# Splitting the first load of a row-mean kernel into eight DMAs of every eighth partition

## Chip, cores, metric

One core of one Trainium2 chip. The metric is device time of one execution in microseconds (us). "Span" is the time from the first to the last instruction in the profiled execution; it is some 2 us shorter than the device time. Every run in this document ran in the fast state at full clock. The kernel before repeats within some 0.3 us (one of its 46 runs beside the other kernels was 0.6 us above its median), so that differences of tenths of a us can be read when they recur. Profile views are cut to the lines that matter; code is cut where a comment says so.

## The reference

```python
def setup_inputs():
    batch, dim = 1024, 4096
    return {"x": np.random.randn(batch, dim).astype(np.float32), "axis": -1}

def reference(x, axis):
    mean = np.mean(x, axis=axis, keepdims=True)
    return ((x - mean) ** 2).astype(np.float32)
```

16.78 MB come in and 16.78 MB go out, with two cheap passes over the data between: it is a job for the DMA engines.

## The kernel before

Four rows of the input lie side by side in one partition, so that one half of the input is a tile of 128 partitions with 64 KiB in each. There are two such tiles; both are loaded at once, and each is stored in two halves as soon as its rows are done.

```python
    P, Q, H = 128, 4, 2
    ntiles = B // (P * Q)                       # 2
    x_t = x.rearrange("(n p q) d -> n p (q d)", p=P, q=Q)
    # ... out_t likewise, pools cut ...
    for i in range(ntiles):
        x_tile = io.tile([P, Q * D], F32)       # 128 x 16384: 64 KiB in each partition
        nc.sync.dma_start(out=x_tile, in_=x_t[i])
        tiles.append(x_tile)

    for i in range(ntiles):
        for q in range(Q):
            row = tiles[i][:, q * D:(q + 1) * D]
            # neg_sum = -sum(row) on VectorE; neg_mean = neg_sum / D; row = Square(row + neg_mean) on ScalarE (cut)
            if q % H == H - 1:
                part = slice((q + 1 - H) * D, (q + 1) * D)
                nc.sync.dma_start(out=out_t[i][:, part], in_=tiles[i][:, part])
```

Of the kernel before, what the change touches and what calls it, by code (L numbers as in the profile page):

```python
# [2 lines left out]

os.environ.setdefault("NEURON_RT_ULTRASERVER_MODE", "4")

# [4 lines left out]

F32 = mybir.dt.float32


@with_exitstack
def kernel(
    ctx: ExitStack,
    tc: tile.TileContext,
    x: bass.AP,
    axis: bass.AP,
    out: bass.AP,  # L20
):


    nc = tc.nc

    B, D = x.shape
    P = nc.NUM_PARTITIONS
    Q = 4
    H = 2
    assert B % (P * Q) == 0  # L30
    ntiles = B // (P * Q)
    inv_d = 1.0 / float(D)

    x_t = x.rearrange("(n p q) d -> n p (q d)", p=P, q=Q)
    out_t = out.rearrange("(n p q) d -> n p (q d)", p=P, q=Q)

    io = ctx.enter_context(tc.tile_pool(name="io", bufs=ntiles))
    stats = ctx.enter_context(tc.tile_pool(name="stats", bufs=2 * ntiles * Q))

    tiles = []  # L40
    for i in range(ntiles):
        x_tile = io.tile([P, Q * D], F32)
        nc.sync.dma_start(out=x_tile, in_=x_t[i])  # L43
        tiles.append(x_tile)

    for i in range(ntiles):
        for q in range(Q):
            row = tiles[i][:, q * D:(q + 1) * D]
            neg_sum = stats.tile([P, 1], F32)
            neg_mean = stats.tile([P, 1], F32)  # L50
            nc.vector.reduce_sum(  # L51
                out=neg_sum, in_=row, axis=mybir.AxisListType.X, negate=True
            )
            nc.vector.tensor_scalar_mul(out=neg_mean, in0=neg_sum, scalar1=inv_d)  # L54
            nc.scalar.activation(  # L55
                out=row,
                in_=row,
                func=mybir.ActivationFunctionType.Square,
                bias=neg_mean,
                scale=1.0,  # L60
# [6 lines that stand above are left out]
# [1 line left out]
_INS = ['x', 'axis']  # L68
_OUTS = [((1024, 4096), 'float32')]

_NUMBERS = {'axis': -1}


# [26 lines left out]
```

## Time and profile before

| | before |
|---|---|
| device time, median of 3 runs | 83.3 us (83.25 to 83.38) |
| span | 81.3 us |
| busy: VectorE, ScalarE | 35.4 us, 30.7 us |
| share of the DMA engines' time filled by packets | 96.2% |
| first load landed, second load landed (start of the reduction that waits for it) | 22.50 us, 41.83 us |
| one load packet (one partition's 64 KiB, on one of 16 DMA engines) | 2.418 us, 27.1 GB/s |

Read it from the last row upwards. Sixteen engines at 27.1 GB/s make 434 GB/s, and 33.55 MB at that rate take 77.3 us of the 81.3. The packet times come from the trace's records of single transfers; sixteen packets run side by side, and I call sixteen of them a *round*. A load is eight rounds. Nothing but the stream of rounds sets the time.

### The profile page before, as it was taken

The numbers are of one execution on the slowest core, as the hardware profiler recorded it, in microseconds if no ns is written. First come the engines' busy times: TensorE is split into PE (matmuls) and PEld (weight loads), VectorE is DVE, ScalarE is ACT, GpSimd is POOL, SyncE is SP. The second block draws the span as 40 slices with busy tenths as digits, with TensorE's granted clock in tenths as the row PEclk, the third lists the DMA queues.
The fourth block names the chain that finished last, engine by engine and source line by source line (L and its number), as shares of the span: only waits on it lengthen the run. The fifth ranks groups of instructions, "written<-read, shape, count | busy, mean of one in ns | idle before, by whom it ended". The sixth has DMA issues, their size and how long they took to land.

```text
span 81.3 us, 79 instructions
## 1 busy us (share of the span) xinstructions
DVE 35.4 (44%) x16; ACT 30.7 (38%) x9; POOL 0.2 (0%) x4
## 2 busy tenths in 40 slices
DVE  0000000000099999999749999999920000000000
ACT  0000000000060005969699930979879980000000
POOL 0000000000000000000000000000000000000000
DMA  9399947999965999992997997997998998898990
GB/s 387 129 516 516 516 193 322 516 516 516 516 290 226 516 516 516 516 483 129 419 516 306 467 516 322 451 516 338 435 516 354 419 516 387 387 516 387 403 500 0
DMA packets 864, 33.55 MB, mean 413 GB/s; under 512 B 96, under 2 KB 96, under 8 KB 96
## 3 DMA queue, kind: packets, MB, share of 16 engines
q1 hardware_dynamic: 864, 33.55, 96.2%
HBM read 16.78 MB, written 16.78 MB: 412 GB/s over the span
## 4 chain that ended last, share of the span: by engine, by line
DMA 50%; DVE 22%; ACT 5%; ACTq 4%; SPq 0%; issue 0%
DMA x_tile<-in_x_dram 50%; DVE neg_sum L51 21%; ACT x_tile L55 5%; ACTq L95 4%; SPq L43 0%; DVE neg_mean L54 0%
## 5 line engine op out<-in xcount | busy, mean ns | idle before, releaser
L51 DVE TENSOR_REDUCE neg_sum<-x_tile 128x1 f32<-128x4096 f32 x8 | 35.0, 4413 | 24.1 <-DMA x_tile<-in_x_dram 24.1
L55 ACT ACTIVATE x_tile<-x_tile,neg_mean 128x4096 f32<-128x4096 f32 x8 | 29.4, 3704 | 13.5 <-DVE neg_mean L54 13.5
L55 ACT ACT_TABLE_LOAD x1 | 1.3, 1283 | 22.5 <-DMA x_tile<-in_x_dram 22.5
L54 DVE TENSOR_SCALAR neg_mean<-neg_sum 128x1 f32<-128x1 f32 x8 | 1.1, 148 | 0.0
L81 POOL MEMSET const-bfloat16-1.0<- 128x1 bf16 x1 | 0.1, 101 | 0.0
L81 POOL MEMSET const-uint8-127<- 128x1 uint8 x1 | 0.1, 101 | 0.0
L81 POOL MEMSET const-float32-0.0<- 128x1 f32 x1 | 0.1, 98 | 0.2 <-issue 0.2
L81 POOL MEMSET const-float32-1.0<- 128x1 f32 x1 | 0.1, 98 | 0.0
## 6 DMA issues: line engine op xcount, KB each, us to landing
out_dram<-x_tile SPq DMA_DIRECT2D x4, 4096.0 KB, 12.9
x_tile<-in_x_dram SPq DMA_DIRECT2D x2, 31.2
```

What stands on the lines that cost most here:

```text
L51: nc.vector.reduce_sum(out=neg_sum, in_=row, axis=mybir.AxisListType.X, negate=True)
L54: nc.vector.tensor_scalar_mul(out=neg_mean, in0=neg_sum, scalar1=inv_d)
L55: nc.scalar.activation(out=row, in_=row, func=mybir.ActivationFunctionType.Square, bias=neg_mean, scale=1.0,)
L81: nc = _bacc.Bacc("TRN2", target_bir_lowering=False, num_devices=1)
L95: with _tile.TileContext(nc) as tc:
```

## The change

The first of the two loads becomes eight DMAs. DMA number g takes partitions g, g+8, ..., g+120: sixteen rows of 64 KiB, one for each DMA engine. The bytes, the row length and the number of rows per engine stay as they were; a plausible intent is to have many transfers in flight while each keeps all sixteen engines at work and spans the whole tile.

```diff
     H = 2
+    G = 8
@@
         x_tile = io.tile([P, Q * D], F32)
-        nc.sync.dma_start(out=x_tile, in_=x_t[i])
+        if i == 0:
+            for g in range(G):
+                nc.sync.dma_start(out=x_tile[g::G, :], in_=x_t[i][g::G, :])
+        else:
+            nc.sync.dma_start(out=x_tile, in_=x_t[i])
         tiles.append(x_tile)
```

## The prediction

It was written before the changed kernel had run. Its main account, to which it gives some 0.85, assumes that the sixteen rows of a small DMA share by twos the rate of one row (27.1 GB/s). That was the author's estimate: no trace of the kernel before shows it, where every row from the second round on takes 2.42 us.

> **What bounds the kernel now.** I read the page first, from the top down to the chain that ended last.
>
> ```profile
> span 81.3 us, 79 instructions
> DVE 35.4 (44%) x16; ACT 30.7 (38%) x9; POOL 0.2 (0%) x4
> ...
> DMA  9399947999965999992997997997998998898990
> GB/s 387 129 516 516 516 193 322 516 516 516 516 290 226 516 516 516 516 483 129 419 516 306 467 516 322 451 516 338 435 516 354 419 516 387 387 516 387 403 500 0
> ...
> q1 hardware_dynamic: 864, 33.55, 96.2%
> HBM read 16.78 MB, written 16.78 MB: 412 GB/s over the span
> ```
>
> No compute engine is busy half of the span, while the packets of the one DMA queue fill 96.2% of the sixteen transfer engines' time. The low digits in the two DMA rows are no gaps: a whole round of packets is booked at its end. In the trace's own packet records, the 256 load packets (65,536 B each) follow one another without a hole on every engine, 2.418 us each after a first round of 3.06 us, and the store packets (32,768 B, 1.213 us each) follow the last load at once, up to 80.2 us. So the kernel is one unbroken stream of 33.55 MB. Next I asked who waits for it, then the timeline.
>
> ```profile
> DVE neg_sum L51 <- DMA x_tile<-in_x_dram: 24.1, 2, 22.5
> ...
> SPq L64 <- ACT x_tile L55: 43.1, 4, 16.9
> SPq L64 <- DMA x_tile<-in_x_dram: 20.9, 1, 20.9
> ```
>
> ```profile
> 0.73 0.86 SPq L43 DMA_DIRECT2D x_tile<-in_x_dram  x2
> 22.50 8.75 DVE L51 TENSOR_REDUCE neg_sum<-x_tile 128x1 f32<-128x4096 f32 x2 [22.50 <-DMA x_tile<-in_x_dram]
> ...
> 39.46 27.65 SPq L64 DMA_DIRECT2D out_dram<-x_tile  x4
> ...
> 41.83 8.75 DVE L51 TENSOR_REDUCE neg_sum<-x_tile 128x1 f32<-128x4096 f32 x2 [1.62 <-DMA x_tile<-in_x_dram]
> ```
>
> Both loads are issued by 1.6 us. The first lets VectorE start at 22.50 us, the second at 41.83 us. The difference, 19.33 us for 8.39 MB, is 434 GB/s: the full rate of the stream. The first store is issued at 39.46 us, 2.4 us before the second load has ended, so it queues behind it. Compute sits between the loads and the stores but never starves the queue; the end is set by bytes over rate. A change matters only if it slows the stream or opens a hole in it.
>
> [...]
>
> **The change part by part.** *What stays.* The same 128 rows of 64 KiB, 8 per engine, the same bytes; every compute instruction; the stores. The instruction order of the two kernels differs on SyncE alone: eight 16-partition copies replace one of 128. In its waits, the first reduction, the table load and the first store now wait for eight semaphores, and the second load waits for the first small one, whose semaphore it reuses.
>
> *Issue.* The two issues on the timeline took 0.86 us, 0.43 each. Seven more are 7 x 0.43 = 3.0 us, all but the first beside transfers that are running: an engine's row takes at least 2.42 us, the next issue is there after 0.43. On the path: 0. The second load is issued after the first small one has landed[...], when each engine has about six rows still to do. On the path: 0.
>
> *Waits.* Seven more semaphore waits ahead of the first reduction[...] go into the 2.4 us by which the first store is early. On the path: 0.
>
> [...]Here is the cost. DMA number g writes partitions g, g+8, ..., g+120. [...] An engine works its rows in order, so the sixteen stay in step[...]. [...]two rows need 2 x 2.418 = 4.84 us. Eight rounds: 8 x 4.84 = 38.7 us against 8 x 2.418 = 19.3 us in the kernel before. Cost: +19.3 us, all of it on the path, since the stream has no hole. The first reduction moves from 22.5 to about 41.9 us, the second load's end from 41.8 to about 61, and stores follow it as now; the first store stays some 2 us ahead of it.
>
> *Sum.* 83.3 + 19.3 + 0 = 102.6 us. I take off 0.2: the engines start 0.5 us apart (packet starts 1.75 to 2.27 us in the trace)[...]. Predicted 102.4 us.
>
> **The rivals.**
> *A: it is hidden, same time.* [...] Outcome 83 to 85.5 us.
> *B: sharing is unfair.* If one engine of a pair is served first, [...]it needs 4 x 2.418 us per half, its partner runs one half behind, and the first load takes three halves of 9.7 us, 29 us, instead of four. The leading engine could even begin its share of the second load. Outcome 88 to 96 us. Nothing in the profile speaks for it; the packets before differ by 2 ns.
> *C: a wait or the issue becomes the bound.* Eight small DMAs, each with its own completion, could leave holes at their borders, or the reused semaphore hold the second load up. Against it: issue is 0.43 us against rows of 2.42 us or more, and the queue is eight rows deep. If each border still cost 0.3 us, that is +2.4 us on top.
> *D: faster.* All eight parts are awaited before any compute starts, so no work can begin earlier. I see no way but noise.
>
> **Range and chances.** [...]within it the spread is small, since it is a count times a measured packet time[...]. B takes 0.04, A 0.10, D 0.01. The range 100 to 104.5 holds the main account and leaves A and B outside. Chances: faster 0.01, same 0.09, slower 0.90 (the last part of A, up to 85.5 us, counts as slower).
>
> **What would show it right or wrong.** Right: the span grows to about 100.5 us with the busy times of VectorE and ScalarE unchanged; the longest wait of the first reduction is about 42 us instead of 22.5; GB/s over the first 41 us is near 215, while the DMA busy digits stay high (packets take 4.84 us, they are not missing); after that 430 GB/s as before; the distance from the first to the second load's end stays 19.3 us. [...] B shows as a first reduction near 32 us with load packets of uneven length; C as DMA digits with holes in the first 40 us, or a second load that ends much later than 19.3 us after the first. The time is wrong also if stores start late: then SyncE's wait for ScalarE, not the queue, would stand before the first store with the DMA idle.

## The result

| | before | after |
|---|---|---|
| device time, median of 5 | 83.35 us (83.25 to 83.40) | 104.73 us (104.64 to 104.92) |
| ratio after/before | | 1.2573, interval 1.2556 to 1.2590 |
| span | 81.3 us | 102.9 us |
| first reduction starts | 22.50 us | 44.17 us |
| first reduction of the second tile starts | 41.83 us | 63.28 us |

A ratio here is the mean time of one kernel's fast runs over that of the other's of the same rounds, so not quite the ratio of the medians quoted. The change costs 21.4 us. The direction and the rough size were predicted; the median lies 0.2 us above the stated range of 100 to 104.5.

The page of the kernel after, the same parts as in the prediction (busy time, the two DMA rows in 40 slices of the span, and the queue's packets, MB and share):

```profile
span 102.9 us, 97 instructions
DVE 35.4 (34%) x16; ACT 30.7 (30%) x9; POOL 0.2 (0%) x4
...
DMA  9290909090909090999999999999999999999990
GB/s 356 51 407 0 407 0 407 0 407 0 407 0 407 0 407 0 407 407 407 407 407 407 407 407 407 407 407 407 471 522 433 407 407 407 407 407 484 522 420 0
...
q1 hardware_dynamic: 976, 33.56, 96.4%
```

VectorE and ScalarE are busy exactly as long as before. The packets still fill 96.4% of the engines' time: nobody idles. But in the first sixteen slices every second slice shows 407 GB/s and the next 0, some 204 on average (a round is booked at its end, and a round now lasts two slices of 2.57 us). A DMA busy share near 100% therefore says nothing about the rate; the GB/s row does. From slice 17 on the old rate is back. The windows of the two kernels say the same in one number each (columns: window, busy times of the compute engines, clock, DMA share, GB/s); first before, then after:

```profile
3.00:18.00 15.00, 0.00 (x0) 0.00 (x0) 0.00 (x0) 1.00 0.97 419
```

```profile
3.00:18.00 15.00, 0.00 (x0) 0.00 (x0) 0.00 (x0) 1.00 1.03 210
```

The waits and the timeline of the kernel after:

```profile
DVE neg_sum L56 <- DMA x_tile<-in_x_dram: 45.6, 2, 44.2
...
SPq L48 <- DMA x_tile<-in_x_dram: 2.8, 1, 2.8
```

```profile
0.73 5.00 SPq L46 DMA_DIRECT2D x_tile<-in_x_dram  x8
8.57 0.34 SPq L48 DMA_DIRECT2D x_tile<-in_x_dram  x1
...
44.17 8.74 DVE L56 TENSOR_REDUCE neg_sum<-x_tile 128x1 f32<-128x4096 f32 x2 [44.17 <-DMA x_tile<-in_x_dram]
...
61.13 27.43 SPq L69 DMA_DIRECT2D out_dram<-x_tile  x4
...
63.28 8.74 DVE L56 TENSOR_REDUCE neg_sum<-x_tile 128x1 f32<-128x4096 f32 x2 [1.40 <-DMA x_tile<-in_x_dram]
```

The new wait of the second load for the first small DMA (2.8 us) ends at 8.57 us, when each engine has six rows still to do; it costs nothing. All of the loss is in the first wait: 44.2 us instead of 22.5. The second tile follows 19.1 us behind the first, as before, and the first store is again issued before the loads have ended. In the transfer records the rounds of the first load took these mean times in us:

```
round            1     2     3     4     5     6     7     8   | first round of the second load
before         3.06  2.42  2.42  2.42  2.42  2.42  2.42  2.42 | 2.42
after          4.77  5.10  5.11  5.11  4.96  5.11  5.11  5.11 | 2.84
```

Twice 2.42 us would be 4.84. The rounds doubled, as predicted, and then some: that surplus of 0.27 us a round is what put the time outside the range.

### The profile page after: what moved, and what is told of

It reads as the page before. It is cut to its first block, busy times and chain, and to the rows that moved or that the text cites. A ratio compares the mean times of both kernels' runs of the same rounds, so it can differ in the third digit from the quotient of the medians.

```text
span 102.9 us, 97 instructions
## 1 busy us (share of the span) xinstructions
DVE 35.4 (34%) x16; ACT 30.7 (30%) x9; POOL 0.2 (0%) x4
## 3 DMA queue, kind: packets, MB, share of 16 engines
q1 hardware_dynamic: 976, 33.56, 96.4%
## 4 chain that ended last, share of the span: by engine, by line
DMA 38%; DVE 34%; SPq 4%; ACT 4%; ACTq 3%; another core or an unknown queue 1%; issue 0%; DVEq 0%
DMA x_tile<-in_x_dram 38%; DVE neg_sum L56 34%; SPq L46 4%; ACT x_tile L60 4%; ACTq L100 3%; DVE neg_mean L59 0%; DVEq L56 0%
```

## The experiments

Theories on the table: *partitions* (the partitions that are written together decide the rate; the prediction's account, with sixteen rows eight partitions apart at half rate) against *the number of DMAs as such*; and for the surplus of 0.27 us: *sharing* itself loses it, each DMA's *border* costs it, or the *source* rows, read 512 KiB apart, are slower. All kernels gave the right result unless the text says otherwise. The transfer records give each row's start, time and size, but do not name the engine: engines are told apart here by which row follows which, and their numbers in the expectations are the author's. A *pair* is the author's word for two rows in flight that share the rate of one; except in one_pair, the records do not show which rows would be one. Medians are compared with the kernel before on the same chip.

| run | first load, or what is put ahead of it | us | before | ratio |
|---|---|---|---|---|
| halves | 2 DMAs: partitions 0-63, 64-127 | 104.54 | 83.17 | 1.256 |
| cols8 | 8 DMAs: 128 partitions x 2,048 columns | 84.66 | 83.17 | 1.017 |
| probe_step8 | 4 extra DMAs of 16 rows, partitions g, g+8, ... | 103.74 | 83.17 | 1.247 |
| probe_step4 | 4 extra DMAs of 16 rows, partitions 32+g, 36+g, ... | 93.22 | 83.17 | 1.120 |
| blocks16 | 8 DMAs of 16 neighbouring partitions | 138.76 | 83.28 | 1.664 |
| blocks32 | 4 DMAs of 32 neighbouring partitions | 104.13 | 83.28 | 1.250 |
| alternate | the change, order 0, 4, 1, 5, 2, 6, 3, 7 | 103.58 | 83.28 | 1.244 |
| near_source | the change, reading neighbouring rows | 104.77 | 83.28 | 1.258 |
| stagger | alternate, engines set off against each other | 107.31 | 83.28 | 1.290 |
| short32 | the change, packets of 32 KiB | 104.82 | 83.28 | 1.259 |
| step4 | 4 DMAs of every fourth partition | 83.73 | 83.28 | 1.005 |
| step2 | 2 DMAs of every second partition | 83.54 | 83.28 | 1.004 |
| one_pair | 4 extra DMAs of 2 rows, neighbouring partitions | 102.02 | 83.30 | 1.225 |
| one_pair_own | 4 extra DMAs of 2 rows, partitions g, g+4 | 94.12 | 83.30 | 1.133 |
| probe_step7 | 1 extra DMA of 16 rows, partitions 11, 18, ..., 116 | 86.21 | 83.30 | 1.036 |
| alternate32 | alternate, 16 DMAs of 32 KiB rows | 101.96 | 83.30 | 1.225 |
| four_pairs | 4 extra DMAs of 8 rows, partitions g, g+8, ..., g+56 | 103.28 | 83.23 | 1.239 |
| four_pairs_alone | the same, other engines idle at first | 103.47 | 83.23 | 1.241 |

### Is it the partitions written? probe_step8 and probe_step4

The cleanest pair: the kernel before with four extra loads into a spare buffer that nothing reads. The two kernels have the same source rows, 16 rows a DMA, the same number of DMAs; only the partitions written differ.

```diff
+    extra = spare.tile([P, Q * D], F32)
+    for g in range(4):
+        nc.sync.dma_start(out=extra[g::8, :], in_=x_t[0][g::8, :])           # probe_step8
+        nc.sync.dma_start(out=extra[32 + g:96:4, :], in_=x_t[0][g::8, :])    # probe_step4
```

> The kernel before with four more loads ahead of it, into a spare buffer that nothing reads: 16 rows each, partitions g, g+8, ..., as in the change (g = 0 to 3). Result stays right. Sharing, border and source theory alike: four rounds of 5.1 us, 83.4 + 20.4 + 0.4 for the later start = 104.2 us.

> The same four extra loads with the same 16 source rows each, but into partitions 32+g, 36+g, ..., 92+g (step 4)[...]. Sharing theory: four rounds of 2.42 us, 83.4 + 9.7 + 0.4 = 93.4 us. Border theory: 4 x 0.27 more, 94.5 us. Source theory (the reads are the same 512 KiB apart): 94 to 94.5 us. If any DMA of 16 rows is slow, whatever its partitions: 104.2 us.

The view of the issuing line: first each kernel's issues (count, shortest/median/longest ns, first and last start), then the time from issue to landing. First probe_step8, then probe_step4:

```profile
L43 SPq DMA_DIRECT2D extra<-in_x_dram x4: 561/576/589, 0.7 to 2.6; - x4
...
DMA to landing us min/median/max: 8.1/14.8/21.5
```

```profile
L43 SPq DMA_DIRECT2D extra<-in_x_dram x4: 568/579/589, 0.7 to 2.6; - x4
...
DMA to landing us min/median/max: 5.2/7.9/10.6
```

Between the first and the fourth landing pass 21.5 - 8.1 + 1.9 (the later issue) = 15.3 us for three rounds, 5.1 us each, against 10.6 - 5.2 + 1.9 = 7.3 us, 2.4 us each. The times, +20.6 and +10.1 us, are near those expected if the partitions decide (104.2 and 93.4 us, +20.8 and +10.0). The number of rows, issues, completions and the distance of the source rows are the same in both, so none of them is the cause. The partitions written are; nothing else in the two kernels differs.

### Does it take the step of four? probe_step7

probe_step4 tried one set of sixteen partitions. Step 7 from 11 is another set, with no step of four or eight in it.

```diff
+    nc.sync.dma_start(out=extra[11:11 + 7 * 16:7, :], in_=x_t[0][0::8, :])
```

> The kernel before with one extra load of 16 rows ahead of it, into partitions 11, 18, ..., 116 (step 7) of a spare buffer[...]. [...]one more round of 2.42 us, its first packets about 3.1 us, 83.3 + 2.4 + 0.4 = 86.1 us. [...]first packets near 4.8 us, 88.5 us or more.

The extra round took 3.05 us, as the first round of the kernel before (3.06), and the time grew by 2.9 us, as expected for a full-rate round (86.1 us; 88.5 for a slow one). So it does not take the step of four: sixteen rows seven partitions apart are as fast.

### The count of DMAs, and neighbouring partitions: halves, blocks16, blocks32, cols8

```diff
-            for g in range(G):
-                nc.sync.dma_start(out=x_tile[g::G, :], in_=x_t[i][g::G, :])
+            for g in range(2):    h = slice(64 * g, 64 * g + 64)   # halves;  blocks32: 4 x 32;  blocks16: 8 x 16
+                nc.sync.dma_start(out=x_tile[h, :], in_=x_t[i][h, :])
+            for g in range(8):    c = slice(2048 * g, 2048 * g + 2048)   # cols8
+                nc.sync.dma_start(out=x_tile[:, c], in_=x_t[i][:, c])
```

> First load as two DMAs, partitions 0-63 and 64-127 ([...]only two completions[...]). Sharing theory ([...]5.11 us a round): 8 x 5.11 = 40.9 us of loading, time near 104.3 us. Border theory (sharing is an exact 4.84 us, the missing 0.27 us a round is paid at each small DMA's completion): 8 x 4.84 + 2 x 0.27, near 103 us. Source theory (the missing part comes from reading rows 512 KiB apart): near 102.6 us. [...]

> First load as eight DMAs of 16 neighbouring partitions[...]. [...]rounds of 9.67 us, 77.4 us of loading, time near 141.5 us. Sharing theory with the loss seen with two engines[...]: rounds of 10.2 us, 81.8 us, time near 146 us. A loss that grows with the sharers: above 148 us. [...]small DMAs as such: near the 104.7 us of the change.

> First load as four DMAs of 32 neighbouring partitions[...]. If the loss in sharing[...]: 5.11 us a round, 104.4 us as with the halves. [...]4.84 us a round, near 102.4 us.

> First load as eight DMAs of 128 partitions x 2,048 columns: as many DMAs, issues, completions and waits as in the change[...]. [...]no sharing, so 83.4 to 84 us. Border theory: 8 x 0.27 = 2.1 us more than before, near 85.5 us. If the number of DMAs as such were the cost: near 104 us.

Two DMAs of 64 neighbouring partitions (halves) lose as much as the eight of the change, 21.4 us, with rounds of 5.12 us. So the surplus isn't paid at the borders of small DMAs: there are two of them here. blocks32, with 32 neighbouring partitions a DMA, has rounds of 5.11 us as well. With 16 neighbouring partitions (blocks16) the round is 9.32 us. This is the landing view of blocks16, whose eight DMAs land 9.3 us apart ((73.5 - 11.9 + 3.5) / 7):

```profile
L47 SPq DMA_DIRECT2D x_tile<-in_x_dram x8: 382/420/682, 0.7 to 4.2; - x8
...
DMA to landing us min/median/max: 11.9/42.9/73.5
```

9.32 us is *less* than four times 2.418, 9.67: the sixteen rows together moved 112.5 GB/s, a little more than a quarter of 434. My 141.5 us (four times 2.418 us a round) and my 146 us (twice 5.11) were both too high, and that this round would be a whole multiple of the full-rate one was an estimate that did not hold.

cols8, with as many DMAs as the change but each over all 128 partitions, costs 1.5 us, between the two expectations. It isn't a clean control, and I do not read the 1.5 us as the price of eight DMAs: its columns arrive in order, so compute starts at 8.1 us and the first store is issued at 21.4 us and joins the loads. What it does show is that eight DMAs as such do not cost 20 us, and that an early start of compute gains nothing in a kernel whose stream has no hole.

### Does the small DMA have to be slow? step4 and step2

```diff
+            for g in range(4):   # step4; step2: range(2), g::2
+                nc.sync.dma_start(out=x_tile[g::4, :], in_=x_t[i][g::4, :])
```

> First load as four DMAs of 32 rows, partitions g, g+4, ...[...]. If an engine takes neighbouring rows of the list (rows 2e and 2e+1, partitions 8e+g and 8e+g+4)[...]: rounds near 4.9 us, 103.5 us. [...]83.7 us.

> First load as two DMAs of 64 rows, every second partition[...]. If engine e takes rows 4e to 4e+3 of the list (partitions 8e to 8e+7, every second)[...]: rounds of 5.11 and 4.9 us in turn, 104 us. [...]83.7 us.

The reduction that waits for the first load, in the timelines of step4 and then of halves (a stepped and a contiguous split):

```profile
23.11 8.74 DVE L56 TENSOR_REDUCE neg_sum<-x_tile 128x1 f32<-128x4096 f32 x2 [23.11 <-DMA x_tile<-in_x_dram]
```

```profile
44.29 8.74 DVE L57 TENSOR_REDUCE neg_sum<-x_tile 128x1 f32<-128x4096 f32 x2 [44.29 <-DMA x_tile<-in_x_dram]
```

Full rate in step4 and step2, rounds of 2.42 us. The slow outcomes, expected if an engine took neighbouring rows of the list (103.5 and 104 us), did not come; how the rows of a DMA of 32 or 64 are dealt out to the engines the records do not show. The change falls between the two cases: it spans the tile, but in steps of eight, with one row for each engine, and its rounds take 5.11 us. Why steps of eight are slow where steps of four and two are not is not shown.

### Where do the surplus 0.27 us come from? near_source, short32, alternate, alternate32

```diff
+ near_source: in_=x_t[i][16 * g:16 * g + 16, :]                 (wrong result on purpose: rows permuted)
+ short32:     dma_start(..., max_dma_last_dim=32768)
+ alternate:   for g in (0, 4, 1, 5, 2, 6, 3, 7)
+ alternate32: for g in range(4): for c in two column halves: for r in (g, g + 4): x_tile[r::G, c]
```

> The change with the same partitions written, but each DMA reads 16 neighbouring rows of the input (64 KiB apart, not 512 KiB). Wrong result on purpose: the rows of the first half come out permuted. Source theory (part of the 5.11 us comes from reading far apart): 4.84 us a round, near 102.6 us. Sharing theory: unchanged at 104.7 us.

> The change with each row cut in two packets of 32 KiB inside the same eight DMAs ([...]same issues, same bytes). If the loss in sharing is a share of the bytes[...]: 2.556 us a packet, time unchanged at 104.7 us. If it is a fixed 0.27 us at the end of each packet: 2.69 us a packet, 8 x 0.27 = 2.2 us more, 106.9 us. If it is paid only where an engine goes over to a new partition: alternately 2.42 and 2.69 us, 104.7 us.

> The change with its eight DMAs in the order 0, 4, 1, 5, 2, 6, 3, 7[...]. If engines stay in step and nothing else: 104.7 us. In both runs so far the one round[...] was shorter (4.92 to 4.96 us against 5.11): [...]6 more such rounds save 6 x 0.15 = 0.9 us, 103.8 us. If pairs drift apart by their start (up to 0.5 us) and gain that at each change: 101 to 103 us.

> The alternate order with every row cut in two 32 KiB halves as DMAs of their own (16 DMAs)[...]. If each change saves a fixed 0.22 us[...]: packets of 2.33 us, 16 of them 37.3 us against 39.1 us, near 101.8 us. If the saving belongs to a change of row or is a matter of bytes: packets of 2.44 us, 103.6 us.

near_source, at 104.77 us, drops the source theory: reading rows 64 KiB apart changes nothing. In short32 the 32 KiB packets take 2.55 to 2.57 us each (5.12 for the row), so the surplus isn't a fixed sum per packet; it goes with the bytes. In alternate every round from the third on is 4.89 us, in alternate32 the 32 KiB packets take 2.35 us on average instead of 2.56. Each change from a DMA with g below 4 to one with g of 4 or more, or back, thus goes with about 0.2 us less, whether it comes every 64 KiB (5.11 - 4.89 = 0.22) or every 32 KiB (2.56 - 2.35 = 0.21), and the row of alternate32, 4.70 us, is even below 4.84. Why such a change shortens the round no record shows. The landing views of the changed order and of the change itself, whose last DMA was issued at 5.1 us in both, give the 1.6 us between them:

```profile
DMA to landing us min/median/max: 7.7/22.5/37.3
```

```profile
DMA to landing us min/median/max: 7.8/23.4/38.9
```

### Can the pairs be separated? stagger

If rows slowed each other only in fixed pairs within one small DMA (the author's assumption), then engines that are one row apart, in the alternate order, would be at work on DMAs g and g+4, and pairs set off like this should run at the full rate. Two extra loads, of 4 and of 12 rows, were to set the engines off.

```diff
+    for k, p0 in ((4, 32), (12, 33)):      # 4 rows, then 12 rows
+        nc.sync.dma_start(out=extra[p0:p0 + 4 * k:4, :], in_=x_t[0][0:k, :])
+            for g in (0, 4, 1, 5, 2, 6, 3, 7): ...     # then as in alternate
```

> The alternate order (0, 4, 1, 5, ...) with two more loads ahead of it into a spare buffer: 4 rows and 12 rows of 64 KiB. [...]rows of 2.42 to 2.8 us[...], 83.3 + 4.8 + 0.4 = 88.5 us, up to 91 if the offset is not a whole row. [...]103.6 us of the alternate order + 4.8 = 108.4 us. [...] Result stays right.

This failed: 107.31 us, near the 108.4 expected if setting the engines off gains nothing, and far from the 88.5 of full-rate rows. In the records four engines start first, at 2.2 to 2.3 us, eight at 3.5 to 3.9, the last four at 5.5 to 6.1. The offset came out only in part. Whichever way these groups of four are matched into pairs, one half of the pairs ran less than 1 us apart and the other half 1.6 to 2.6 us. If each pair had shared in private (half rate only while both are in the same small DMA), row time plus offset would be 4.84 us, so I estimate at most 3.2 us a row (4.84 - 1.64) for the second half; yet once all sixteen were under way every row of every group took 4.4 to 4.6 us. Since probe_step4 and probe_step8 had settled that the partitions written are the reason, this speaks against pairs that are independent of each other; the next runs test that directly.

### Do rows that share slow the others? one_pair, one_pair_own, four_pairs, four_pairs_alone

```diff
+    for g, p0 in enumerate((0, 2, 32, 34)):                                        # one_pair: neighbours
+        nc.sync.dma_start(out=extra[p0:p0 + 2, :], in_=x_t[0][2 * g:2 * g + 2, :])
+        nc.sync.dma_start(out=extra[g:g + 8:4, :], ...)                            # one_pair_own: four apart
+        nc.sync.dma_start(out=extra[g:64:8, :], in_=x_t[0][8 * g:8 * g + 8, :])    # four_pairs: eight apart
+    # four_pairs_alone: g = 0, 1 into tile 0, g = 2, 3 into tile 1, ahead of the loads that overwrite them
```

> The kernel before with four extra loads of two rows each ahead of it (engines 0 and 1 only)[...] (partitions 0 and 1, 2 and 3, 32 and 33, 34 and 35 of a spare buffer). Engines 2-15 go straight to the first real load[...]. [...]engines 2-15 keep rows of 2.42 us, some 400 GB/s in the first 20 us; engines 0 and 1 need 4 x 5.1 us more and end last, near 104 us. [...]rows of 4 to 5 us on all, near 215 GB/s in the first 20 us, time also near 104 us. The GB/s decide, not the time.

> The same four two-row loads, but into partitions g and g+4[...]. All theories: no sharing, engines 0 and 1 carry four more rows of 2.42 us, 83.3 + 9.7 + 0.3 = 93.3 us, full rate throughout.

> The kernel before with four extra loads of eight rows ahead of it, partitions g, g+8, ..., g+56 of a spare buffer[...]. The lone pair took an exact 4.84 us a row, eight pairs 5.11. If the loss grows with the number of pairs that share at once: some 4.95 us a row here, 103.5 us. If sharing is exact as long as other engines run free: 4.84 us, 102.2 us. If any set of several pairs loses the full amount: 5.11 us, 104 us.

> The same four loads of eight rows, two into each of the two real tiles ahead of their real loads, which overwrite them (so the result stays right) and have to wait for the two small ones of the tile. For the first two rows engines 8-15 have nothing to do, for the last two they run beside the pairs. If the loss of eight pairs comes from the pairs alone: the same row time in all four rounds. If it needs other traffic to collide with: 4.84 us in the first two and more in the last two; if free engines beside it help: the other way round.

The GB/s rows of the pages, in 40 slices of some 2.5 us each, of one_pair and then of four_pairs:

```profile
GB/s 52 367 419 367 419 367 419 367 419 419 419 419 419 445 419 524 288 52 52 52 52 52 52 236 432 432 419 458 484 484 432 419 419 419 419 419 419 419 419 26
```

```profile
GB/s 207 0 414 0 414 0 414 0 414 414 414 414 414 414 414 414 414 414 414 414 414 207 207 310 414 414 427 479 427 427 414 414 414 504 427 414 414 427 479 26
```

In one_pair the window from 3 to 18 us runs at 389 GB/s: by the transfer records fourteen engines keep rows of 2.42 to 2.6 us while the two that write neighbouring partitions need 4.83 to 4.85 us after their first row, twice 2.418 us: the two share 27.1 GB/s, the rate of one. (In slices 18 to 23 only these two are left, at 52 GB/s.) One pair is a private matter here. In four_pairs the same window runs at 210 GB/s. Were the eight engines of the real load free and the other eight at half rate as in one_pair, the sum would by my estimate be 8 x 27.1 + 8 x 13.5 = 325 GB/s; instead all sixteen rows in flight take 5.10 to 5.13 us from each engine's second row on, those of the real load included. And four_pairs_alone has rows of 5.07 us for the eight engines even while the other eight have nothing to do, 5.09 beside traffic. So the surplus is there with eight rows eight partitions apart and does not need other traffic, and beside them the rows of the real load are slow as well, which took 2.42 us in the kernel before.

one_pair_own (+10.8 us for four rows more at full rate, 93.3 expected) shows the price of adding rows to two engines alone: four rows of 2.42 us are 9.7 of the 10.8.

What separates one pair from four is open: the number of pairs, or the fact that in one_pair the partitions are neighbours and the rows only two. blocks32 writes neighbouring partitions too and has the full 5.11 us, which speaks for the number. Two or three pairs, or two rows alone eight or more partitions apart, were not run.

## Why the prediction missed

Its account held in nearly every step that the runs could test:

- **What bounds the kernel**: the stream. Confirmed; compute is unchanged and the time grew by what the loads grew.
- **Issue, on the path 0**: wrong by 0.35 us. The later issues are hidden, but the first of them is longer (0.58 us against 0.38, 0.2 us of the 0.35) and the first packet starts at 2.10 us instead of 1.75. I had taken the issue time from the 128-row DMAs.
- **Waits, on the path 0**: right. The first store, at 61.13 us, still goes out ahead of the last load packet's end at 62.8 us.
- **Half rate for sixteen rows eight partitions apart**: right but for the surplus (5.11 us a round, 4.84 predicted), and that the partitions written are the reason is shown by probe_step8 (103.74 us) against probe_step4 (93.22). That the rows share by twos is the author's estimate; the records show the half rate alone.
- **Rivals**: A falls with the result, C with halves: its 0.3 us a border is near the measured 0.27 us a round by chance, for halves has two borders and loses as much. B, one engine of a pair served first, would have given uneven packets; from the second round on they agree within 0.02 us in a round (in the first, with its spread start, they took 4.45 to 5.20 us). What the prediction read against B, "the packets before differ by 2 ns", was too tight a reading: after the first round they took 2.418 to 2.434 us.

**The step that failed is a term of the sum: "two rows need 2 x 2.418 = 4.84 us."** That is what a lone pair does (one_pair: 4.83 to 4.85). The sixteen rows of a small DMA take 5.11 us. The terms, from the transfer records of the two profiled executions:

| term | predicted | measured |
|---|---|---|
| first packet starts later | 0 | +0.35 (2.10 - 1.75) |
| round 1 | +2.42 | +1.71 (4.77 - 3.06) |
| rounds 2 to 8 | +16.93 | +18.69 (35.62 - 16.93) |
| first round of the second load | 0 | +0.42 (2.84 - 2.42) |
| gain of the engines that start ahead | -0.2 | not seen (see round 5 below) |
| rest, not attributed | 0 | +0.2 |
| sum | +19.1 | +21.4 |

The biggest error is rounds 2 to 8, +1.76 us; the late start and the gain that did not come add 0.55 us; the first rounds together cost 0.3 us less than assumed. Round 5, where the order passes from g = 3 to 4, is 0.15 us shorter than its neighbours, but for all sixteen rows alike (4.96 to 4.97 us), whether their engine was ahead or not. That engines ahead gained nothing fits what four_pairs shows: in the first round of the second load all sixteen rows were slow, 3.00 us for the one that began first (42.47 us) down to 2.55 us for the last (43.34 us). In these runs an engine that was ahead did not run at 2.42 us a row while the others were still in the slow rows.

The range was too narrow besides. I called the spread small because the cost was "a count times a measured packet time"; but the packet time had been measured without sharing, and its doubling was an assumption. An assumed size deserves a wider range than a measured one.

What stays open is by which rule partitions hinder each other, why rows eight apart lose some 5% beyond the half (5.11 us against 4.84) and slow everybody, why 16 neighbouring partitions got more than a quarter of the full rate (9.32 us against 9.67) when 32 and 64 got less than half of it (5.11 and 5.12 against 4.84), and how rows are dealt out when a DMA has 32 or 64 of them.

No experiment beat the kernel before. Among the splits of the first load, step2 and step4 come within 0.5% of it; splitting gained nothing here: by partitions, all parts are awaited before the first reduction, and by columns (cols8) the earlier start of compute met a stream that has no hole.

## What to carry to other kernels

Before splitting a load by partitions, write down which partitions the rows that are in flight *together* go to. In these runs they decided the rate, not the number of rows or DMAs: with 16 rows a DMA a round took 2.42 us in steps of four from 32 on, 5.11 in steps of eight, 9.32 for neighbours. Keep 128 partitions in one DMA, or, if it has to be split, split by columns (84.66 us here) or with a step of two or four over the whole tile (83.54 and 83.73 us). And read the GB/s row, not the DMA busy share: a stream at half its rate is as "busy" as one at full rate (DMA share 1.03 at 210 GB/s, 0.97 at 419, from 3 to 18 us).

## Rates and issue times measured here

- Sixteen rows in flight, in steps of eight, carried 205 GB/s (16 rows in 5.11 us) while g stayed below 4 or at 4 and more, 214 when it changed between the two every row (4.89 us), 223 when it changed every 32 KiB (2.35 us a packet). Sixteen neighbouring partitions carried 112.5 GB/s (9.32 us).
- Two DMAs on the two halves took as long as the change (halves: 104.54 us, +21.4). DMAs of 64 and 32 stepped rows (83.54 and 83.73 us) and even of 16 rows (partitions 32, 36, ..., 92; rounds of 2.42 us) ran at the full rate.
- Two rows in neighbouring partitions (one_pair) left the other engines at 2.42 to 2.6 us a row; eight rows eight partitions apart (four_pairs) came with 5.10 to 5.13 us on all sixteen engines.
- The first issue of a kernel took 0.54 to 0.75 us where the DMA had a partition step (first packet at 2.04 to 2.23 us), and 0.38 us where it took 16, 32 or 128 neighbouring rows (first packet at 1.75 to 1.77 us). With 64 neighbouring rows (halves) it took 0.54 us, and a plain 128-row load right behind other DMAs took up to 0.58 us (in halves, step2, step4), so the step alone does not decide it; what does is open.
